# Emission order from a planned time of each operation instead of each stage, matmul kind changes in the planner's clock, and 17 + 23 work buffers instead of 15 + 24

## The chip, the cores and the metric

The kernel runs on one core of one Trainium2 chip. The metric is the device time of one execution in microseconds (us), as the median of several runs of the same program. The engines are named as in the profile: PE is the matrix engine, PEld its weight loads, DVE the vector engine, ACT the scalar engine, POOL the GpSimd engine, and SP the sync engine, which here does nothing but issue DMAs.

## The reference

One layer of a hybrid encoder over a sequence of 512 tokens with a model width of 1024, everything in float32. Cut to what is computed:

```python
h = rmsnorm(x, mix_norm)
p = h @ w_in                                   # 1024 -> 9248 columns
rx, ry, qkv, z, ba, gates = split(p)
y_rnn = rglru_branch(rx, ry, ...) @ w_rnn_proj # conv, two gated scans (forward, backward), gelu gate
y_dn  = deltanet_branch(qkv, z, ba, ...) @ w_dn_proj
g_rnn, g_dn = split(sigmoid(gates))
x = x + (g_rnn * y_rnn + g_dn * y_dn) @ w_out
h = rmsnorm(x, ffn_norm)
gt, up = split(h @ w_gate_up)                  # 1024 -> 2 * 2816
x = x + (silu(gt) * up) @ w_down
return rmsnorm(x, final_norm)
```

`deltanet_branch` is a chunked gated delta rule for 8 heads and two directions. Within a chunk it solves a triangular system (`lhs = A + eye`), and it carries a 128 x 128 state per head and direction from chunk to chunk.

## The kernel before, in words

**How it computes.** Each float32 operand of a large product is split into two parts, a rounded one (`hi`, type float32r) and the rest (`lo`), and a product is three matmuls: hi x hi, hi x lo and lo x hi. These "float32r" matmuls have 512 or 256 columns. ACT makes `hi` (a cast) and DVE makes `lo` (a subtraction) from a raw weight tile that SP has loaded. The two largest parts of the feed-forward block, `gate_up` and `down_first`/`down_second`, and `w_out`, are Strassen-like products with 7 instead of 8 block products, for which DVE also forms sums of blocks. The triangular inverse in `dn_inverse` (L924) is made of small float32 matmuls with `tile_position`, on 32 x 32 and then on 64 x 64 pieces of the array; the delta rule itself (`dn_mats`, L884, and `dn_state`, L1008) uses plain float32 matmuls of 128 or 256 columns; transposes are matmuls with the identity. So PE sees four kinds of work: float32r matmuls, transposes, full-size float32 matmuls, and small float32 matmuls on parts of the array.

**`dn_inverse`, which the prediction returns to.** It runs once for each of four groups `g` of two heads. Each run issues four sets of small matmuls: `pr` (32 of 32 x 32, L963 to L969), then `px` (32) and `pz` (16), both 32 x 32 and both fed by the same tile `R`, which ACT makes from `pr` (L972 to L980), then `pr2` (16 of 64 x 64, L992) and `px2` (16 of 64 x 64, L999). Between one set and the next lies an ACT operation that reads the PSUM of the first, except between `px` and `pz`. In the trace each float32 matmul has two rows, so a set of 32 shows as 64.

**How the order is made.** Nothing is issued while `trunk` (L390) runs through the code. Every operation goes through a recorder (`Rec`, L325), which gives it an engine, a cost in ns from a formula by operation and size, its dependences and the tiles it touches, and hands it to `Plan.add` (L123). At the end `Plan.order` (L150) plays the whole program against a clock of its own: each engine that is free picks, among its operations whose dependences are done, the one with the lowest number in `when` (`pick`, L225); it is busy for the operation's cost; a dependent operation becomes ready after a lag from the table `LAG`. The sequence in which operations were picked is the order of emission on each engine, and each engine of the chip then executes its list strictly in that order.

**Where `when` comes from.** `spend` (L444) cuts the program into 216 stages. The list `TIMES` (L35) holds one hand-over number for each stage, in units of 100 ns, between -163526 and 246650. They are priorities and not clock times. An operation's `when` is its stage's number plus an offset inside the stage (L154 to L161), so all operations of a stage, say all small matmuls of one `dn_inverse`, stand together.

**Tile promises.** Most tiles come from pools with a fixed number of buffers: `t2` (tag of `two`, 2 KB in each partition, `N2` buffers), `t4` (tag of `four`, 4 KB in each partition, `N4` buffers), `wraw` and `wx` (weights, 4 each), and three tags of PSUM banks, `mm` (3), `ax` (3) and `st` (2). An operation that needs a new tile can be picked only when `slots` (L192) allows it: a buffer must be free, and no more may be handed out than leaves room for the tiles with an earlier first use, as judged by `first` and `last` (L167 to L174), the lowest and highest `when` of the operations that touch a tile.

**The queues.** SP issues nearly all loads in the planned order and waits at each for the buffer it writes into. PE has no second queue: what stands in front of its list and is not ready holds everything behind it.

Of the kernel before, what the change touches and what calls it, by code (L numbers as in the profile page):

```python
# [14 lines left out]
P = 128  # L15
# [16 lines left out]
WARM = 3400  # L32
RELEASE = 200
LOOK = 40
TIMES = [  # L35
# [14 lines left out]
]  # L50
ENGINES = ("PE", "DVE", "ACT", "POOL", "SP")
N2, N4, NW = 15, 24, 4
# [7 lines left out]
class Plan:  # L60
# [9 lines left out]

    def __init__(self, nc):
        self.nc = nc
        self.ops = []
        self.where, self.bases = [], []
        self.t = self.base = 0.0
        self.stage = 0
        self.tags = {}
        self.tile_tag = {}
        self.hist = {}
        self.keep = set()  # L80
        self.extra = ()
        self.admit = ()
# [40 lines left out]
    def add(self, eng, fn, outs, ins, cost, tail=0.0, table=None):  # L123
# [23 lines left out]
        self.where.append((self.stage, round(1e3 * (self.t - self.base))))  # L147
        self.bases.append(round(1e3 * self.base))

    def order(self):  # L150
# [4 lines left out]
        when = []  # L155
        for (s, d), b in zip(self.where, self.bases):
            if s < len(TIMES):
                b, b0 = TIMES[s] * 100, b
            elif TIMES:
                b += max(TIMES) * 100 - b0  # L160
            when.append(b + d)  # L161
# [6 lines left out]
        for i, o in enumerate(ops):  # L168
            key = (when[i], i)
            for name in o[3]:  # L170
                if name in self.tile_tag:
                    uses[name] = uses.get(name, 0) + 1
                    first[name] = min(first.get(name, key), key)
                    last[name] = max(last.get(name, key), key)  # L174
# [14 lines left out]
        pe_end, cold = 0, WARM  # L189
# [53 lines left out]
        while True:  # L243
            for e in ENGINES:
# [17 lines left out]
                if e == "PE":  # L262
                    if now - pe_end > 3000:
                        cold = 0
# [60 lines left out]
class Rec:  # L325
# [5 lines left out]
    def __getattr__(self, op):  # L331
        real = getattr(self.real, op)

        def call(*a, **kw):
# [14 lines left out]
            elif e == "PE":  # L349
# [3 lines left out]
                cols = elems(a[1]) if op == "matmul" else P  # L353
                if op == "transpose":
# [1384 lines left out]
```

## Time and profile before

| | |
|---|---|
| median of 3 runs | 1052.06 us (1051.90 to 1052.31) |
| span of the profiled execution, first to last instruction | 1051.0 us |
| of the runs' time outside such a span (median less span) | 1.06 us |
| PE busy | 1037.1 us, 99% |
| PEld busy | 905.0 us, 86% |
| DVE busy | 869.5 us, 83% |
| ACT busy | 706.7 us, 67% |
| granted PE clock, mean | 0.999 |
| read from memory, written | 121.12 MB, 12.09 MB |

How to read the rows that follow: a row of the timeline has the start in us from the span's first instruction, the length, the engine, the line, the operation, what it writes and reads (`mm<-hh,wx`), for PE the piece of the array used (`128*128`, `32*32`), the output's shape, and the number of instructions merged into the row; in brackets, how long the engine sat idle before it and what ended that. All operations are issued from the recorder's one line, L384, so the line number tells nothing here and groups are told apart by tile names and shapes. Tiles are named by their tag: `t` stands for `t2` and `t4`, `ax`, `mm` and `st` for PSUM banks, `na` for the delta rule's matrices and later the residual. Matmuls overlap in the pipe, so a matmul's own length in the trace is longer than the time it takes from PE; that is read from the distance between starts.

### The profile page before, as it was taken

The page shows a single profiled execution, that of the slowest core. Times are in us where ns is not written, and L with a number is a line of the kernel's source. Part 1 is how long each engine was busy: PE and PEld are TensorE (multiplying, and loading weights), DVE is VectorE, ACT ScalarE, POOL GpSimd, SP SyncE. Part 2 cuts the span into 40 slices and gives each one's busy share as a digit, 9 for nine tenths or more (in the row PEclk, how much of TensorE's full clock was granted, in tenths as well). Part 3 has the DMA queues.
Part 4 walks back from the last instruction along what each step waited for, and adds up shares of the span by engine and source line. Part 5 has one row for each costly group of instructions (what it writes and reads, how often), then busy time and mean ns, then how long its engine had stood idle before and what let it go on. Part 6 is the DMA issues. An engine that isn't in the chain of part 4 may idle for free.

```text
span 1051.0 us, 17876 instructions
## 1 busy us (share of the span) xinstructions
PE 1037.1 (99%) x6707; PEld 905.0 (86%) x6707; DVE 869.5 (83%) x1626; ACT 706.7 (67%) x1287; POOL 75.7 (7%) x133
## 2 busy tenths in 40 slices
PE   8999999999999999999999999999999999999997
PEld 7888788888888987887888798889999999998886
DVE  7769989669794697489469657999999898989997
ACT  7799989787537877686875644668544454556574
POOL 2000000204100220211021000000000000000000
PEclk9999999999999999999999999999999999999999
DMA  9622222245233256559536564688453644336532
GB/s 278 196 79 81 61 75 75 71 112 148 81 100 91 73 144 150 158 133 218 122 76 145 169 172 140 197 256 292 129 171 102 200 139 130 109 110 207 197 123 80
DMA packets 180854, 146.95 MB, mean 140 GB/s; under 512 B 6784, under 2 KB 161552, under 8 KB 180768
## 3 DMA queue, kind: packets, MB, share of 16 engines
q1 hardware_dynamic: 175840, 129.95, 41.8%
q0 software_dynamic: 3744, 12.72, 6.5%
q10 hardware_dynamic: 1184, 3.15, 0.8%
q8 instruction: 52, 0.85, 0.3%
q14 instruction: 34, 0.28, 0.1%
HBM read 121.12 MB, written 12.09 MB: 127 GB/s over the span
## 4 chain that ended last, share of the span: by engine, by line
PE 86%; DVE 8%; ACT 2%; DMA 2%; issue 1%; SPq 1%; ACTq 0%; DVEq 0%
PE mm L384 49%; PE ax L384 23%; PE st L384 15%; DVE t L384 6%; ACT t L384 1%; DVE na L384 1%; DVE wx L384 1%; SPq L384 1%; DMA t<-in_w_down_dram 1%; DMA wraw<-in_w_in_dram 1%; DMA gain2r<-in_ffn_norm_dram 0%; ACT wx L384 0%; ACT ax L384 0%; ACTq L384 0%; ACT na L384 0%
## 5 line engine op out<-in xcount | busy, mean ns | idle before, releaser
L384 PE MATMUL mm<-hh,wx 128*128 128x512 f32 (+2 forms) x1280 | 368.8, 363 | 0.1
L384 DVE TENSOR_TENSOR t<-t,t 128x512 fp32r<-128x512 f32 (+25 forms) x501 | 249.3, 511 | 30.3 <-ACT t L384 20.7
L384 PEld LDWEIGHTS mm<-hh,wx 128*128 128x128 f32 (+1 forms) x1280 | 230.4, 188 | 35.4 <-ACT wx L384 0.7
L384 PE MATMUL mm<-hl,wx 128*128 128x512 f32 (+2 forms) x648 | 228.6, 362 | 0.0
L384 ACT CAST wx<-wraw 128x1024 fp32r<-128x1024 f32 (+3 forms) x139 | 129.9, 937 | 90.6 <-PE mm L384 32.9
L384 PE MATMUL ax<-t,t 128*128 128x512 f32 (+3 forms) x1134 | 156.9, 292 | 1.2 <-DVE t L384 1.2
L384 DVE TENSOR_TENSOR wx<-wraw,wx 128x1024 fp32r<-128x1024 f32 (+3 forms) x115 | 120.7, 1051 | 35.5 <-PE mm L384 16.8
L384 PEld LDWEIGHTS ax<-t,t 128*128 128x128 f32 (+1 forms) x1134 | 123.0, 161 | 21.6 <-issue 2.2
L384 PEld LDWEIGHTS mm<-hl,wx 128*128 128x128 f32 (+1 forms) x648 | 121.7, 188 | 16.8
L384 ACT CAST t<-t 128x512 fp32r<-128x512 f32 (+2 forms) x148 | 94.1, 653 | 44.5 <-DVE t L384 36.1
L384 PE MATMUL mm<-t,wx 128*128 128x512 f32 x480 | 116.6, 394 | 0.0
L384 PEld LDWEIGHTS mm<-t,wx 128*128 128x128 f32 x480 | 89.0, 188 | 18.4 <-issue 0.2
L384 DVE SCALAR_TENSOR_TENSOR t<-mm,par,t 128x511 f32<-128x511 f32 (+1 forms) x108 | 80.2, 744 | 20.9 <-ACT t L384 19.7
L384 ACT ACT_TABLE_LOAD x64 | 82.1, 1283 | 5.0 <-DVE t L384 2.3
L384 PE MATMUL mm<-t,t 128*128 128x256 f32 (+1 forms) x420 | 79.8, 330 | 0.1
L384 ACT ACTIVATE t<-t 128x128 f32<-128x128 f32 (+4 forms) x86 | 47.5, 559 | 41.0 <-DVE t L384 39.3
L384 PEld LDWEIGHTS mm<-t,t 128*128 128x128 f32 x420 | 63.8, 190 | 7.2 <-DVE t L384 0.5
L384 PE MATMUL st<-hh,wx 128*128 128x512 f32 (+1 forms) x224 | 67.7, 375 | 0.0
L384 ACT CAST t<-wraw 128x1024 fp32r<-128x1024 f32 (+1 forms) x55 | 49.2, 894 | 18.3 <-DMA wraw<-in_w_gate_up_dram 7.2
L384 DVE TENSOR_TENSOR t<-wraw,t 128x1024 fp32r<-128x1024 f32 (+1 forms) x55 | 56.3, 1023 | 5.3 <-ACT t L384 5.1
L384 PEld LDWEIGHTS st<-hh,wx 128*128 128x128 f32 x224 | 41.2, 188 | 7.6
L384 PE MATMUL st<-hl,wx 128*128 128x512 f32 (+1 forms) x112 | 41.5, 375 | 0.0
(195 smaller groups left out, 1519.1 us busy)
## 6 DMA issues: line engine op xcount, KB each, us to landing
wraw<-in_w_in_dram SPq DMA_DIRECT2D x72, 512.0 KB, 4.1
wraw<-in_w_gate_up_dram SPq DMA_DIRECT2D x44, 512.0 KB, 4.1
wx<-wraw POOLq DMA_DIRECT2D x24, 512.0 KB, 5.3
wraw<-in_w_out_dram SPq DMA_DIRECT2D x12, 512.0 KB, 4.5
wraw<-in_w_rnn_proj_dram SPq DMA_DIRECT2D x16, 384.0 KB, 3.5
t<-in_w_down_dram SPq DMA_DIRECT2D x11, 512.0 KB, 5.9
sums<-t SPq DMA_DIRECT2D x11, 512.0 KB, 5.0
wraw<-sums SPq DMA_DIRECT2D x11, 512.0 KB, 3.6
```

The costliest lines, as they stand in the source:

```text
L384: self.plan.add(e, lambda: real(*a, **kw), outs, ins, cost, tail, table)
```

## The change

The code that computes is untouched; the same 9123 operations are recorded in the same sequence. What differs is the planner.

- `TIMES`, with 216 numbers, gives way to `PLAN`, with 9123 numbers in units of 50 ns from 0 to 26830, one for each operation; `when` is that number. Stage and offset are no longer recorded.
- `first` and `last` of a tile are no longer the lowest and highest `when`. A pass through the dependences, in order of `when` among what is ready, gives each operation a rank, and a tile's first and last rank are used.
- Matmuls get a kind, kept where ACT's operations keep their table: 0 for float32r, 1 for a transpose, 2 for full-size float32, 3 for float32 on a part of the array. Where a matmul follows one of another kind, the planner's clock adds the entry of `TURN`, in ns: 95 from any other kind to kind 3, and from kind 3 back 215 to float32r, 100 to a transpose and 50 to full-size float32. `pick` itself does not look at kinds.
- Two cost formulas change: a small matmul of 64 columns costs 67 instead of 76 ns, and the slow DVE transpose is told by the number of dimensions of its operands instead of by its size.
- `N2` becomes 17 (from 15) and `N4` 23 (from 24). Together they keep 126 KB of each partition, as before.

```diff
-TIMES = [
-    -162283, -159297, -163526, -108037, -92752, -158970, -94346, -59098, 168648, -70151, -72611, -51972, -22916,
...
-]
+PLAN = """
+4054 7177 4989 4992 6589 4992 6593 2272 7050 2718 0 2823 4601 4293 4247 5798 5866 5860 5903 5818 5891 6158 6049 5989
...
+26810 26811 26825 26402 26821 26410 26830
+"""
 ENGINES = ("PE", "DVE", "ACT", "POOL", "SP")
-N2, N4, NW = 15, 24, 4
+N2, N4, NW = 17, 23, 4
...
+    TURN = ((0, 0, 0, 95), (0, 0, 0, 95), (5, 5, 0, 95), (215, 100, 50, 0))
...
-        when = []
-        for (s, d), b in zip(self.where, self.bases):
-            if s < len(TIMES):
-                b, b0 = TIMES[s] * 100, b
-            elif TIMES:
-                b += max(TIMES) * 100 - b0
-            when.append(b + d)
+        when = [50 * int(t) for t in PLAN.split()]
...
         uses, first, last = {}, {}, {}
-        for i, o in enumerate(ops):
-            key = (when[i], i)
-            for name in o[3]:
+        todo, heap = list(left), []
+        for i in range(n):
+            if not todo[i]:
+                heapq.heappush(heap, (when[i], i))
+        rank = 0
+        while heap:
+            i = heapq.heappop(heap)[1]
+            for name in ops[i][3]:
                 if name in self.tile_tag:
                     uses[name] = uses.get(name, 0) + 1
-                    first[name] = min(first.get(name, key), key)
-                    last[name] = max(last.get(name, key), key)
+                    first.setdefault(name, 2 * rank)
+                    last[name] = 2 * rank + 1
+            rank += 1
+            for u in users[i]:
+                todo[u] -= 1
+                if not todo[u]:
+                    heapq.heappush(heap, (when[u], u))
...
                 if e == "PE":
+                    c += self.TURN[mode][o[6]]
+                    mode = o[6]
                     if now - pe_end > 3000:
...
+                table = 1 if op == "transpose" else 0 if not four_ else 3 if elems(a[0]) <= 64 and a[0].shape[0] < P else 2
                 if op == "transpose":
                     cost = 110
                 elif four_:
-                    cost = 22 if cols == 32 else 76 if cols == 64 else n * 4 / 2.4 + 10
+                    cost = n * 4 / 2.4 + 10 if table == 2 else 22 if cols == 32 else 67
...
                 elif op == "transpose":
-                    cost = 68 + (2.0 if n > 512 else 1.1) * n
+                    cost = 68 + (2.05 if len(list(ins[0].ap)) > 3 or len(list(out.ap)) > 3 else 1.1) * n
```

More of the change, by code (lines that the diff above doesn't have):

```diff
@@ L73, in __init__ @@
         self.ops = []
-        self.where, self.bases = [], []
         self.t = self.base = 0.0
@@ L146, in add @@
         self.ops.append((eng, fn, deps, touched, round(cost), round(1.25 * tail), table, self.t))
-        self.where.append((self.stage, round(1e3 * (self.t - self.base))))
-        self.bases.append(round(1e3 * self.base))
     def order(self):
@@ L188, in order @@
         table = None
-        pe_end, cold = 0, WARM
+        pe_end, cold, mode = 0, WARM, 0
         result, start = [], {}
```

477 rows, old and new, of tables (PLAN, TIMES) are left out of this document.

## The prediction

> **What bounds the kernel now.** I read the page's head first, then the table of stretches, then PE's waits.
>
> ```profile
> span 1051.0 us, 17876 instructions
> PE 1037.1 (99%) x6707; PEld 905.0 (86%) x6707; DVE 869.5 (83%) x1626; ACT 706.7 (67%) x1287; POOL 75.7 (7%) x133
> ```
>
> PE is busy 1037.1 of 1051.0 us. An order can shorten only the 13.9 us in which PE is idle, and that part of its busy time which is not work but turning from one kind of matmul to another. So the question is where the 13.9 us lie. In the table of stretches each row has the stretch, its length, busy time (and instructions) of PE, PEld, DVE, ACT, POOL, then clock and DMA:
>
> ```profile
> 0.00:9.77 9.77, 6.40 (x33) 5.99 (x34) 4.90 (x16) 5.51 (x11) 7.04 (x21) 1.00 0.79 275
> 9.77:25.00 15.23, 13.62 (x100) 11.99 (x100) 13.29 (x31) 13.85 (x31) 0.00 (x0) 1.00 1.11 278
> 25.00:320.00 295.00, 294.99 (x1363) 244.40 (x1363) 247.51 (x360) 226.42 (x343) 21.55 (x30) 1.00 0.35 99
> 320.00:635.00 315.00, 313.93 (x2515) 266.55 (x2514) 214.28 (x568) 228.95 (x509) 46.23 (x81) 1.00 0.56 139
> 635.00:940.00 305.00, 303.75 (x2235) 289.69 (x2234) 284.57 (x484) 165.56 (x290) 0.87 (x1) 1.00 0.52 160
> 940.00:1044.00 104.00, 104.00 (x468) 86.26 (x467) 101.82 (x163) 64.55 (x103) 0.00 (x0) 1.00 0.49 159
> 1044.00:1051.10 7.10, 0.37 (x4) 0.17 (x2) 3.17 (x11) 1.85 (x5) 0.00 (x0) 0.85 0.53 192
> ```
>
> Idle of PE by stretch: 3.37 before the first product at 9.77; 1.61 up to 25; 0.01 in the next 295 us; 1.07 in the stretch of the four delta-rule groups (320 to 635); 1.25 in 635 to 940 (output projection, gate and up); nothing in 940 to 1044; 6.73 in the tail behind the last matmuls. The clock is 1.00 while PE works, so nothing is to be had there. The waits say who ended these idle times (total, times, longest):
>
> ```profile
> PE ax L384 <- DMA gain1r<-in_mix_norm_dram: 2.9, 1, 2.9
> PE ax L384 <- DVE t L384: 2.3, 3, 1.2
> PE mm L384 <- DVE hl L384: 1.3, 2, 0.8
> PE mm L384 <- ACT hh L384: 0.2, 1, 0.2
> PE ax L384 <- ACT ax L384: 0.2, 1, 0.2
> ```
>
> Of 6.9 us of waits the first 2.9 is the very first load, ahead of which there is no work. About 4 us remain. That the rest of the busy time is dense is seen in the chain, whose longest pieces are steady runs (start, us, what, matmuls):
>
> ```profile
> 277.53 45.33 PE mm L384 x200
> 812.36 4.32 PE ax L384 x36
> ```
>
> 45.33 / 200 is 0.227 us for a 512-column matmul, 4.32 / 36 is 0.120 for one of 256. A rule of the Trainium skill speaks against reading "99%" as the end: Perfetto Trace Analysis, section Identifying the Most-Contended Engine, calls matmul busy share a poor measure and has one look at the share of weight loads. By it there would be 14% of headroom (86% on the page); the two steady rates, which have no gap to close, say that an order finds none of it.
>
> **Terms of the change. First, the small matmuls.** PE's timeline shows visits to kind 3 between float32r runs (start, length, form, count):
>
> ```profile
> 322.89 0.75 PE L384 MATMUL ax<-t,na 32*32 32x32 f32 x64
> ...
> 324.70 0.75 PE L384 MATMUL ax<-t,t 32*32 32x32 f32 x64
> 325.38 2.56 PE L384 MATMUL mm<-t,wx 128*128 128x512 f32 x10
> 327.87 0.69 PE L384 MATMUL ax<-t,t 32*32 32x32 f32 x32
> 328.50 0.73 PE L384 MATMUL mm<-t,wx 128*128 128x512 f32 x2
> ...
> 419.95 0.75 PE L384 MATMUL ax<-t,t 32*32 32x32 f32 x64
> 422.90 0.69 PE L384 MATMUL ax<-t,t 32*32 32x32 f32 x32
> 500.56 1.02 PE L384 MATMUL ax<-t,t 32*32 32x32 f32 x96
> 501.51 0.50 PE L384 MATMUL mm<-hh,wx 128*128 128x512 f32 x1
> 503.01 1.52 PE L384 MATMUL mm<-hh,wx 128*128 128x512 f32 x6
> 504.46 1.15 PE L384 MATMUL ax<-t,na 64*64 64x64 f32 x32
> 505.54 0.97 PE L384 MATMUL mm<-hh,wx 128*128 128x512 f32 x3
> 506.34 0.39 PE L384 MATMUL mm<-hl,wx 128*128 128x512 f32 x1
> 591.54 1.02 PE L384 MATMUL ax<-t,t 32*32 32x32 f32 x96
> 598.09 1.15 PE L384 MATMUL ax<-na,t 64*64 64x64 f32 x32
> ```
>
> Around a visit: six matmuls from 503.01 should take 1.36 and the visit starts after 1.45, so 0.09 going in; three from 505.54 should take 0.68 and take 0.80, so 0.12 coming out. Inside there is a fixed part too: 64 rows take 0.68 (324.70 to 325.38), 32 take 0.63 (327.87 to 328.50), 96 together 0.95 (500.56 to 501.51). So `px` and `pz` as two visits cost 0.68 + 0.63 + 0.21 more of turning, 1.52, and as one 0.95: **a needless visit costs 0.57 us**. Groups 0 and 1 split the two sets (64 + 32), groups 2 and 3 don't (96). There are 18 visits from 322.89 to 598.09, 5 + 5 + 4 + 4. Four a group is the least, since ACT stands between the sets. In the diff the numbers (in us, 50 ns each) of the `pz` sets begin below those of `px` in three groups (the third has 798.95 us against 790.65), so `pz` no longer queues behind. I take both joins: 2 x 0.57 = **-1.1**, between -1.1 and a gain of nothing.
>
> All 18 visits have float32r on both sides. Coming out into a plain float32 matmul is planned as cheaper; no row shows it. Between 0 and 18 x 0.12 = -2.2 (the way out, gone altogether). I take 0, as `pick` doesn't look at kinds, and keep -1.9 for the 16 visits as an end.
>
> The Trainium skill, TensorEngine Tiling (Array Packing), section Key Properties, says that changing the tiling mode drains the engine. By that rule each visit pays twice, whatever its size, and the trace agrees with its 0.57. The diff's clock charges 0.31 (95 + 215 ns): it knows of the cost but prices it at little over half.
>
> **Second, the start.** SP now issues (start, length, tiles):
>
> ```profile
> 0.80 0.86 SPq L384 DMA_DIRECT2D t<-in_x_dram  x2
> 1.71 0.43 SPq L384 DMA_DIRECT2D wraw<-in_w_in_dram  x1
> 2.18 1.12 SPq L384 DMA_DIRECT2D t<-in_x_dram  x2
> 4.76 2.44 SPq L384 DMA_DIRECT2D wraw<-in_w_in_dram  x2
> ```
>
> `PLAN` puts the first three weight loads (306.20, 306.35, 307.55 us on its scale) ahead of the last two quarters of x (307.65, 307.75). All are ready at once, so the two x loads move behind one load of 128 KB and one of 512 KB. The DMA engines are full here (1.11, 278 GB/s), so x comes some 2.3 us later (640 KB / 278). PE needs these quarters last of all, and three weight tiles on the first half of the tokens are 3 x 24 matmuls of 0.120, 8.6 us of other work. I set the delay at 0 behind that cover; without it, it costs 2.3. In return PE starts with more weights to choose from while `hl` comes slowly (the 1.3 of waits above). Of 0.45 + 1.61 us idle I take **-0.6**, between -2.1 and +2.3.
>
> **Third, the waits in the middle.** 1.07 + 1.25 = 2.32 us. The longest one:
>
> ```profile
> 892.67 0.62 ACT L384 CAST t<-wraw 128x512 fp32r<-128x512 f32 x1 [3.63 <-DMA wraw<-in_w_gate_up_dram]
> 897.64 1.58 PE L384 MATMUL ax<-t,t 128*128 128x256 f32 x11 [1.18 <-DVE t L384]
> ```
>
> ACT sat 3.63 us for a weight load that SP issued late, and five us on PE paid 1.18 for it. A number for each operation can put such a load forward; one for a stage moves the whole stage. The two stretches with 0.01 and 0.00 idle show that a nearly waitless order exists for these costs. Between 0 and -2.3; I take **-1.5**, nearer to those rows. Late next is DVE: 101.82 of 104.00 after 940.
>
> **What I cost at nothing.** Turning between float32r, transposes and full-size float32 (planned at 0 to 5 ns). The tail of 6.73: `PLAN` keeps the sequence of the last eight DVE operations, with the last reciprocal behind the two scalings of another chunk. `marks` now also lists matmuls, as these have a kind; but each of them feeds a sigmoid that it listed already, so no wait is added. The two DVE and matmul formulas act only through the order. Two more `t2` and one fewer `t4`: no row shows a wait by pool, nearest is SP's wait for DVE to let go of a tile (total, times, longest):
>
> ```profile
> SPq L384 <- DVE t L384: 195.5, 72, 7.7
> ```
>
> I take 0, because PE idled 4 us while SP waited 195.5; the bad end is a rival below.
>
> **Sum.** -1.1 - 0.6 - 1.5 = -3.2 on the span of 1051.0, so 1047.8. The median of the runs, 1052.06, lies 1.06 above the span, which the order does not touch: 1047.8 + 1.06 = **1048.9 us**. Everything at its best is -1.1 - 1.9 - 2.1 - 2.3 = -7.4, or 1044.7.
>
> **Rivals.**
>
> *The gain is given back (0.17).* DVE becomes the wait: in 940 to 1044 it is busy 101.82 of 104.00 us, and PE has no slack there either. If the new order gains before 940 by pushing DVE's parts of later weights back, DVE enters this stretch with more to do and PE waits there. Against it: DVE has 20.4 us free in 635 to 940. It takes back from 2 to all of the 3.2: 1050.9 to 1052.1.
>
> *The small sets fall apart: slower (0.15).* With one number for a stage, a set of small matmuls stood together. With a number each, any float32r matmul that is ready and has a number between theirs goes between them. The diff's numbers do spread: the first group's `pr` set from 599.00 to 634.15 us, with 146 float32r matmuls numbered in between; the third group's `px` over 13 us with 60. The set holds together only where all its numbers lie before those of the float32r work then waiting, that is, where the chain comes late. Each split costs 0.57 on the chip and 0.31 in the plan, so the plan may accept some. It decides from 6 extra visits (3.4 us eat the gain); at 10, with the joins lost, it is -2.1 + 5.7 = +3.6, 1055.7. This is the case in which the drain rule above is the whole story.
>
> *One t4 buffer fewer: slower (0.10).* A raw tile is held longer, SP issues later, ACT and DVE get gate and up weights late. Each such event costs about the 1.18 seen once at 897.64, and there are 20 `gate_up` steps. Three more events undo the gain; five make it 1054.8.
>
> **Numbers.** The forecast has 0.58 with 1044.7 to 1050.4. From these: a measurement here can tell 0.2%, 2.1 us, from no change, so faster means below 1049.96 and slower above 1054.16. Of the 0.58, 0.54 is faster, 0.04 is same; of the giving back, 0.02 and 0.15; of the split sets 0.13 slower and 0.02 same; of the buffers 0.07 slower, 0.03 same. Sum: faster 0.56, same 0.24, slower 0.20. The range runs from the best of all terms, 1044.7, to the split sets at ten, 1055.7, beyond which and below which 2 in 10 are left.
>
> **What would show it.** Right: 16 visits to small forms, all `px` with `pz` as 96 rows; PE's waits after 25 us under 1 us in all; PE busy about 1 us less; the tail still 6.7. Wrong: more than 18 visits; a PE wait over 1 us for ACT or DVE; idle PE after 940; a first product later than 9.8, or PE waiting for `hh` around 20 us because x came late.

## The result, and the profile after

The changed kernel takes 1066.18 us (median of 4 runs, 1064.39 to 1068.55), the kernel before 1051.98 us beside it. The ratio is 1.0138, with a 95% interval of 1.0121 to 1.0154: 14.2 us slower, where 3.2 us less was forecast. The profiled execution of the changed kernel took 1067.54 us; its span, first to last instruction, is 1065.8. The head of its page:

```profile
span 1065.8 us, 17804 instructions
PE 1044.2 (98%) x6707; PEld 906.8 (85%) x6707; DVE 870.0 (82%) x1626; ACT 716.0 (67%) x1292; POOL 73.3 (7%) x133
```

PE does the same 6707 matmuls and is busy 7.1 us longer (1037.1 before), and idle 21.6 us instead of 13.9. The table of stretches (columns as in the prediction; the first edge is the first product, the last ones the end of the matmuls):

```profile
0.00:10.79 10.79, 6.40 (x33) 5.91 (x34) 5.21 (x16) 5.73 (x12) 7.14 (x21) 1.00 0.89 226
10.79:25.00 14.21, 12.37 (x97) 11.60 (x98) 11.44 (x28) 10.56 (x24) 0.00 (x0) 1.00 0.95 279
25.00:320.00 295.00, 292.66 (x1339) 240.18 (x1338) 246.00 (x355) 231.16 (x352) 17.89 (x32) 0.99 0.36 99
320.00:635.00 315.00, 309.43 (x2455) 260.74 (x2454) 207.41 (x539) 225.04 (x487) 47.35 (x79) 0.99 0.56 136
635.00:940.00 305.00, 303.92 (x2206) 287.99 (x2205) 280.62 (x494) 168.00 (x299) 0.87 (x1) 1.00 0.53 164
940.00:1059.00 119.00, 119.00 (x585) 100.15 (x584) 116.44 (x188) 73.33 (x116) 0.00 (x0) 1.00 0.43 142
1059.00:1066.00 7.00, 0.48 (x4) 0.27 (x3) 2.84 (x11) 2.14 (x5) 0.00 (x0) 0.74 0.62 222
```

Idle of PE is now 4.39 us before the first product (3.37 before), 1.84 to 25 us (1.61), 2.34 in 25 to 320 (0.01), 5.57 in 320 to 635 (1.07), 1.08 in 635 to 940 (1.25), none to the end of the matmuls, and 6.52 behind them (6.73). So the middle (25 to 940 us), where 1.5 us were to be gained, lost 6.7: 9.0 us of idle in place of 2.3. PE's waits (total, times, longest) name many causes with one wait each:

```profile
PE ax L842 <- issue: 3.7, 1, 3.7
PE ax L842 <- DMA gain1r<-in_mix_norm_dram: 3.0, 1, 3.0
PE mm L842 <- DVE hl L842: 1.8, 3, 1.1
PE st L842 <- DVE wx L842: 1.4, 1, 1.4
PE mm L842 <- ACT wx L842: 1.3, 2, 0.8
PE ax L842 <- DVE t L842: 1.3, 1, 1.3
PE mm L842 <- ACT t L842: 0.9, 1, 0.9
```

The longest, "issue", is one in which PE waited for no other engine. PE's timeline around it, in group 1:

```profile
429.40 0.75 PE L842 MATMUL ax<-t,na 32*32 32x32 f32 x64
...
431.44 1.19 PE L842 MATMUL ax<-t,t 32*32 32x32 f32 x88
436.37 0.33 PE L842 MATMUL ax<-t,t 32*32 32x32 f32 x8 [3.73 <-issue]
...
437.78 1.97 PE L842 MATMUL ax<-t,na 64*64 64x64 f32 x32
```

The joined `px` and `pz` set of 96 rows stops after 88, stands still for 3.73 us, and the 64-wide set behind it takes 1.97 instead of the 1.15 of the kernel before: half clock.

The second thing to see is on ACT, which PE's waits don't show. ACT's waits for transfers, the first rows, before:

```profile
ACT t L384 <- DMA wraw<-in_w_gate_up_dram: 7.2, 6, 3.6
ACT t L384 <- DMA wraw<-in_w_in_dram: 1.9, 2, 1.3
```

and after:

```profile
ACT t L842 <- DMA wraw<-in_w_gate_up_dram: 14.7, 13, 3.6
ACT wx L842 <- DMA wraw<-in_w_in_dram: 12.7, 9, 2.9
ACT wx L842 <- DMA wraw<-in_w_gate_up_dram: 11.6, 2, 7.5
```

Added up over all rows of that view, ACT waits for transfers 19.7 us in 18 waits before, and 57.3 us in 40 waits after. The planner's own clock says the same: of the 272 SP transfers whose first user is ACT or DVE, 41 land under 0.3 us ahead of that use in the order before, 69 in the changed one; the median lead falls from 5.8 to 3.1 us. In the changed order more weights are taken up as they land. One thing speaks against reading too much into this: 33.8 of ACT's 57.3 us (15.0 of the 19.7 before) lie in 635 to 940 us, where PE's idle did not rise.

A number used from here on: the time on the chip less the planner's own end (the instant at which its loop has done the last operation). It is 1051.98 - 1039.3 = 12.7 us for the kernel before and 1066.18 - 1042.7 = 23.5 us for the changed one. The planner itself gives the new order 3.4 us more, the chip another 10.8. The two distances are not quite alike: the planner of the kernel before does not price its turns between matmul kinds, that of the changed one does.

### The profile page after: what moved, and what is told of

Read it like the earlier page. It is cut to its first block, busy times and chain, and to the rows that moved or that the text cites. A ratio compares the mean times of both kernels' runs of the same rounds, so it can differ in the third digit from the quotient of the medians.

```text
span 1065.8 us, 17804 instructions
## 1 busy us (share of the span) xinstructions
PE 1044.2 (98%) x6707; PEld 906.8 (85%) x6707; DVE 870.0 (82%) x1626; ACT 716.0 (67%) x1292; POOL 73.3 (7%) x133
## 4 chain that ended last, share of the span: by engine, by line
PE 78%; ACT 7%; DVE 5%; DMA 4%; issue 2%; ACTq 0%; SPq 0%; DVEq 0%; POOLq 0%
PE mm L842 44%; PE ax L842 22%; PE st L842 13%; ACT t L842 4%; DVE t L842 3%; DVE wx L842 1%; DMA wraw<-in_w_in_dram 1%; ACT wx L842 1%; ACT L842 1%; DMA wraw<-osums 1%; DMA osums<-wraw 1%; DMA wx<-wraw 1%; ACT na L842 1%; DMA t<-osums 0%; DMA wraw<-in_w_dn_proj_dram 0%
## 5 line engine op out<-in xcount | busy, mean ns | idle before, releaser
L842 PE MATMUL mm<-hh,wx 128*128 128x512 f32 (+2 forms) x1280 | 379.4, 365 | 0.9 <-ACT wx L842 0.8
L842 DVE TENSOR_TENSOR t<-t,t 128x512 fp32r<-128x512 f32 (+17 forms) x501 | 251.0, 513 | 26.4 <-ACT t L842 16.4
L842 PEld LDWEIGHTS mm<-hh,wx 128*128 128x128 f32 (+1 forms) x1280 | 233.5, 190 | 37.0 <-ACT wx L842 1.6
L842 PE MATMUL ax<-t,t 128*128 128x512 f32 (+3 forms) x1134 | 172.6, 291 | 4.2 <-issue 3.7
L842 PEld LDWEIGHTS ax<-t,t 128*128 128x128 f32 (+1 forms) x1134 | 126.9, 161 | 24.2 <-issue 4.6
L842 PE MATMUL mm<-t,wx 128*128 128x512 f32 x480 | 123.4, 396 | 1.4 <-ACT t L842 0.9
L842 PE MATMUL mm<-t,t 128*128 128x256 f32 (+1 forms) x420 | 92.1, 329 | 0.0
L842 PEld LDWEIGHTS mm<-t,t 128*128 128x128 f32 x420 | 69.1, 190 | 7.1
L842 PE MATMUL st<-hh,wx 128*128 128x512 f32 (+1 forms) x224 | 70.2, 377 | 1.4 <-DVE wx L842 1.4
L842 POOL TENSOR_SCALAR_AFFINE_SELECT t<-t 128x512 f32<-128x512 f32 x32 | 24.7, 775 | 271.3 <-DMA t<-gcr 233.9
```

The costliest lines, as they stand in the source:

```text
L842: self.plan.add(e, lambda: real(*a, **kw), outs, ins, cost, tail, table)
```

## The experiments

Theories. *Late code*: the single stall of 3.73 us and the half clock behind it, some 6 to 7 us, are half of the loss (PE stands because its next instructions have not arrived). *No slack*: the table's order takes operands up as they are promised, so that any lateness reaches PE, and a wait that is taken away comes back elsewhere. Rivals of the prediction: one `t4` buffer fewer, and sets that fall apart. The second is out at once: there are 16 visits. The first stays untested: one more `t4` buffer (4 KB a partition) does not fit beside the 17 + 23, and with the old 15 + 24 the planner finds no order for this table.

The times of the changed order scatter by 4 us and more (1064.4 to 1068.6; the kernel before 1050.4 to 1053.3 in all its runs), so effects of 1 to 3 us are read from the traces, each of one execution. The runs are called e1 to e16 below.

**Code, by a shift of PE's stream (e1).**

```
+            if i == 2253:
+                for j in range(48):
+                    plan.again(2253 + j % 16)   # same matmul, one column
             plan.ops[i][1]()
```

> The changed kernel with its order untouched; ahead of the 64-wide set that began at 345.73 us, PE gets 48 extra matmuls of one column (into the set's own tile, overwritten by the set), 96 instructions more in PE's stream. Theory of the late code: PE's instructions arrive in blocks of 256, and the block that ends inside group 1's joined set (429.4 to 432.4 us) was used up in 2.8 us, before the next had been fetched. 96 instructions later in the stream that block holds matmuls of 0.227 us as well and lasts 6 to 8 us: the idle of 3.73 us at 436.37 goes, the half clock after it (437 to 441 us, some 3 us of PE time) too, the extra matmuls cost 0.6 to 1.0 us; 1066.2 - 3.7 - 3.0 + 0.8 = about 1060.3 us, unless the blocks at 514 and 602 us (5.6 and 3.2 us by my count after the shift) come late in their turn. Rival: the idle belongs to the place in the order (a transfer, a PSUM bank, a wait that the trace doesn't name): it stays at the same matmul of the set with 3 to 4 us, and the time is 1067 us.

Measured 1069.74 us. The set of 96 no longer stops; the stall has moved on by about the shift, into the next set, and a second one appears at 608 us (1.83 us):

```profile
431.79 1.25 PE L848 MATMUL ax<-t,t 32*32 32x32 f32 x96
...
433.64 0.91 PE L848 MATMUL ax<-t,na 64*64 64x64 f32 x22
437.50 0.56 PE L848 MATMUL ax<-t,na 64*64 64x64 f32 x10 [2.95 <-issue]
```

So it belongs to PE's stream of instructions and not to a place in the order; that the shift would clear it was wrong. Page part 3 has the queue that brings this code:

```profile
q8 instruction: 52, 0.85, 0.3%
```

52 packets of 16 KB for 13,414 matmuls and weight loads, 258 each. From 429.40 to the stop PE ran 64 + 5 + 88 matmuls with as many weight loads, 314 instructions in 3.2 us, more than a packet holds. The packet for which it waited began at 433.76 and took 1.00 us; PE went on 1.6 us after it had landed. In the seven such stalls of the changed kernel and the first five runs it went on 1.3 to 1.6 us after the landing. Counted from the start, PE had begun 4801 or 4802 matmuls and weight loads when it went on, in the changed kernel, in e2 to e5 and in the other plans e12, e14 and e15, and 5058 and 7618 in e1: each time 193 or 194 more than a multiple of 256. This ties the stall to the blocks of code, whatever the order. The Trainium skill (Runtime: NRT & Kernel Launch, section Instruction fetch mechanics) describes blocks of 256 instructions, read ahead by a queue of the engine's own; the trace agrees. It also says that the fetch is hidden by the pace of issue; here it isn't, 3.73 us of PE stand open.

**One wait, by one place in DVE's queue (e2).**

```
+        todo = move(todo, [1803], 2033)   # low half of wx443, ahead of two others
```

> The changed kernel; one DVE operation, the low half of a weight tile (wx443), is emitted ahead of the dn_mats and rg_rest operations that stood before it, so it can begin some 1.5 us earlier (248.9 instead of 250.45 us). Theory of the new wait: PE's wait of 1.44 us at 251.69 is this one queue position; it goes, and with it the eight matmuls at 0.427 instead of 0.227 us behind it (1.6 us): 1066.2 - 3.0 = 1063.2 us, and PE's slip against the planner's clock between 240 and 262 us grows by under 1 us instead of 3.7. Rival, no slack anywhere: the two operations that are now 1.2 us later are waited for in their turn within the next 20 us, and the time stays at 1065 to 1067 us.

Measured 1067.33 us. The wait at 251.69 is gone, and PE waits 1.02 us at 250.17 for the next `wx` of DVE. Matmul for matmul PE is 4.2 us ahead of the changed kernel's trace at 428 us, and 1.0 behind it at 705, after waits of 1.88 us at 617.7 and 1.85 at 700.5, which there are 0.69 and under 0.2. This is what the rival, no slack, said of the time, but the gain at 428 us is not this edit's. In e4 and e5 below, which leave this place as it was, the same wait is 0.28 and 0.32 us (1.50 in e1); they are 4.8 and 4.1 us ahead at 428 us and level with the changed kernel at 705. So the wait changes from execution to execution, and what these three had gained by 612 us they had given back by 705.

**The start (e3).**

```
+        todo = move(todo, [67, 68], 129)   # last quarters of x ahead of the 2nd weight
```

> The changed kernel; SyncE's first loads go back to the order of the kernel before: both last quarters of x ahead of the second weight load (they were issued at 6.58 and 8.40 us, they would be at about 2.2 and 2.8 us). Everything else in the changed order. Theory of the start: the second quarter of x no longer shares the transfer with two more weights (first transposes on it at 9.4, before 8.66 us), and DVE and ACT no longer wait for the late quarters (16.57 and 15.24 us): PE's slip at 60 us falls from 4.3 to about 2.3 us, 1066.2 - 2.0 = 1064.2 us. Rival: the casts of the two weights, now later in the transfer, stand ahead of the hh and hl writes on ACT (9.96 us) and wait instead: the start is the same or longer, 1066 to 1068 us.

Measured 1069.47 us. The rival's mechanism again, on ACT and then on PE:

```profile
11.77 0.41 ACT L842 CAST wx<-wraw 128x256 fp32r<-128x256 f32 x1 [2.62 <-DMA wraw<-in_w_in_dram]
```

```profile
12.61 0.49 PE L842 MATMUL mm<-hh,t 128*128 128x256 f32 x1 [2.60 <-ACT hh L842]
```

The load is late now, its cast stands ahead of the `hh` writes on ACT, and PE waits for these.

**The order inside the joined sets (e4).**

```
+        for a in (2174, 2948, 3756, 4598):
+            run = range(a, a + 48)
...
+            todo = done + [a + 1, a, *run[2:]] + [i for i in todo[k:] if i not in run]
```

> The changed kernel; within each of the four joined px and pz sets (96 rows of 32x32 matmuls) the matmuls stand in the order of the program, px and pz in alternation, instead of the 16 of pz first and then the 32 of px. Theory of the shuffled sets: each joined set falls from 1.4 to the 1.15 us that the joined set at 500.56 us took in the kernel before, so PE is about 0.3 us shorter per set, 1.2 us in all: 1065.0 us; since group 1's set then ends its block of code a little earlier, the idle at 436.37 us may grow by as much as it gains there (0.3 us). Rival: what a set costs is its number of rows and the two turns of kind, not its order: 1066.2 us, no difference that can be measured.

Measured 1069.78 us. The sets do get shorter; the changed kernel first, then this one:

```profile
339.70 1.26 PE L842 MATMUL ax<-t,t 32*32 32x32 f32 x96
340.89 0.73 PE L842 MATMUL mm<-t,wx 128*128 128x512 f32 x2
```

```profile
334.74 1.02 PE L842 MATMUL ax<-t,t 32*32 32x32 f32 x96
335.69 0.73 PE L842 MATMUL mm<-t,wx 128*128 128x512 f32 x2
```

From the start of the set to the next matmul 1.19 us became 0.95, for all four about 1 us. The time doesn't show it: the code stall is 4.30 us here, and idle of PE in all is 16.0 us (gaps between matmuls; 12.3 in the changed kernel).

**The transfers around the late code (e5).**

```
+        todo = move(todo, [3564], 3565)   # a write of 512 KB, one load later
```

> The changed kernel with one SyncE transfer moved: the 512 KB write of sums to DRAM that it issued at 427.99 us is issued one load later, after 431 us. What the four runs before showed: wherever the late block of code fell, PE went on 1.3 to 1.6 us after the block's packet had landed, and the packet itself began 3.6 to 4.7 us after PE had crossed into its last block there, against 0.5 to 0.7 us at the dense set near 339 us, where no transfer was under way. Theory of the queue for transfers: at 430 us a PoolE store, this write and a weight load (three times 512 KB) are in flight and the code's packet stands behind them; without the write it begins 1 to 2 us sooner, the idle in group 1's set falls from 3.7 (2.9 to 4.3) to between 1.5 and 2.5 us, and the time by as much: about 1064.5 us, within what these runs scatter. Rival: the delay of the packet is PE's own (its request goes out late, when the sequencer has run dry): idle and lateness stay at 3 to 4 us.

Measured 1068.16 us; the packet of code came 3.5 us late and PE idled 3.11 us. The transfers behind the write moved up: when PE crossed into its last block, a store by POOL and a weight load were in flight, and the code was as late. That clears this write, and tells nothing of transfers at large: inconclusive.

**One part alone: the joins, in the kernel before (e6).**

```
+        for a, b in ((2174, 2222), (2948, 2996)):
+            k = todo.index(a)
+            todo = [i for i in todo[:k] if not a <= i < b] + list(range(a, b)) \
+                 + [i for i in todo[k:] if not a <= i < b]
```

> The kernel before, with one part of the change alone: in groups 0 and 1 the 16 matmuls of pz are put beside the 32 of px (one set of 96 rows in the order of the program), so two visits fewer, 16 instead of 18; everything else as before. Theory of my first term: two visits at 0.57 us go, 1051.9 - 1.1 = 1050.8 us. Rival of the late code: the denser set uses up its block sooner and an idle of 1 to 4 us opens in it, as in the changed kernel: 1052 to 1056 us.

Measured 1050.77 us against 1052.04 us, ratio 0.9987 (0.9978 to 0.9997): 1.27 us less, where 1.1 was worked out. Groups 0 and 1:

```profile
324.12 1.02 PE L384 MATMUL ax<-t,t 32*32 32x32 f32 x96
325.07 3.03 PE L384 MATMUL mm<-t,wx 128*128 128x512 f32 x12
...
418.84 1.02 PE L384 MATMUL ax<-t,t 32*32 32x32 f32 x96
419.79 1.19 PE L384 MATMUL mm<-hh,wx 128*128 128x512 f32 x4
```

0.95 us a set and no stall. This agrees with the first term, count and price, though the interval allows a gain of 0.3 to 2.3 us; it is faster than both kernels. By the drain rule of the Trainium skill (TensorEngine Tiling (Array Packing), Key Properties) a visit costs whatever its size; two visits fewer and 1.27 us less agree with that.

**Lateness of every weight.** Two burdens, each on both kernels (e7 and e8, e10 and e11).

```
+                to, src = a[0][0:16], a[1][0:16]
+                self.plan.add(e, lambda: (real(to, src), real(*a, **kw)), outs, ins, cost, tail, table)
```

> The changed kernel, each of its 231 weight loads preceded on SyncE's queue by a second load of its first 16 partitions (64 KB, overwritten by the load itself), so every weight lands roughly 0.5 us later; order untouched. Theory of no slack: the changed order takes weights up as they land (the planner's own clock has 69 of 272 loads land under 0.3 us ahead of their first use, 41 before; ACT waits for transfers 57.3 us in 40 waits, 19.7 us in 18 before), so lateness goes straight through ACT's queue to PE: at least 8 us slower than itself, 1074 us or more, and at least one and a half times what the same burden costs the kernel before. Rival: its losses are the late code and half clock alone; it loses what the kernel before loses, within 2 us.

> The kernel before with the same burden on each weight load (64 KB more ahead of it, each weight some 0.5 us later). Theory of no slack in the changed order: this one has more, so it loses 2 to 6 us: 1054 to 1058 us. Rival: both lose the same, whatever that is.

Measured 1322.55 us, and 1249.15 us for the kernel before. The burden was eight times what I meant: the second transfer to the same place waited for the first to land, some 4 us per weight. The sizes were missed, and so was the ratio: the changed kernel lost 256 us, the kernel before 197, 1.30 where at least 1.5 was expected. So, without a byte to spare for waiting:

```
+                parts = [(a[0][p:q], a[1][p:q]) for p, q in ((0, 16), (16, P))]
+                self.plan.add(e, lambda: [real(*x, **kw) for x in parts], outs, ins, cost, tail, table)
```

> The changed kernel, each of its 231 weight loads issued as two transfers, 16 partitions and then the other 112: no byte more, but one more issue on SyncE (some 0.45 us) ahead of most of the load, so the weights land roughly 0.5 us later. (The burden tried before was 4 us per load, since the second transfer to the same place waited for the first; it cost the kernel before 197 us and the changed one 256 us.) Theory of no slack: the changed order passes lateness on more than the one before, in the ratio 1.3 or above: 4 us or more beyond what the kernel before loses under the same burden. Rival: both lose the same within 2 us.

> The kernel before with the same split of its weight loads, 0.5 us later each. Theory of no slack in the changed order: it loses 2 to 10 us, at least 4 us less than the changed kernel loses. Rival: the same loss within 2 us.

Measured 1087.34 and 1066.28 us: the changed kernel loses 21.2 us, the kernel before 14.4 (more than the 10 that I allowed it). The difference, 6.8 us, and the ratio, 1.47, are those that no slack expected; as the runs scatter by 8 and 4 us, the difference is known to some 4 us only. The burden is not quite the same either: the main part of a `w_in` load took 4.8 us to land where the whole took 3.9 (median) in the changed kernel, 4.6 for 4.1 in the kernel before.

Where the time goes is read by setting each profiled execution, matmul for matmul, against that of the same kernel unburdened. The changed kernel is 1.4 us later at 25 us, 2.4 at 635 and 15.7 at the end; the kernel before 2.0, 4.6 and 11.1. So the changed order is the more sensitive one behind 635 us, where the change itself lost nothing. Between 25 and 635 us, where it lost most, the burden cost it 1.0 us, and the kernel before 2.6. The pair shows an order with less slack; it does not show that late weights made the 14.2 us.

**Without the crowd in group 1 (e9).**

```
+            if 2948 <= i < 2996 or 3010 <= i < 3026:
+                if i in (2948, 2949, 3010):
...
+                    nc.tensor.matmul(plan.sets[1][k][:, 0:n], sl[0:1, :], f(hh[0:1, 0, 0:n]), start=True, stop=True)
+                continue
             plan.ops[i][1]()
```

> The changed kernel without the crowd in which code came late: of group 1, the joined px and pz set (96 rows) and the 64-wide set after it are left out, each of their three tiles is filled with zeros by one matmul instead (so that group's inverse is not computed; ACT's copies and everything after them run as before), and PE's stream is 244 instructions shorter, about one block, so later sets lie in their blocks as before. Own work: 96 rows at 1.4 us and the 64-wide set at 1.3 us go, three fp32 matmuls of 256, 256 and 512 columns come (0.43 + 0.43 + 0.85 us): 1.0 us less. Theory of the late code: with it go the idle of 2.9 to 4.3 us and some 3 us at half clock: 1066.2 - 1.0 - 3.7 - 3.0 = about 1058.5 us. Theory of no slack: PE comes to 445 us that much sooner, and waits for ACT's weights and transfers instead, between 560 and 710 us above all (0.7 to 2.2 us each, as in the runs where it came there 4 us sooner): 1062 to 1066 us, with 3 us or more of new waits of over 0.6 us behind 445 us.

Measured 1063.45 us, 2.7 less than the changed kernel. Little of it is work left out: the matmuls that fill the tiles took 1.05 and 1.05 us (1.7 in all were expected), the two sets take 1.19 and 1.08 where nothing stops them. No stall for code is left. In its place, PE's longest waits:

```profile
PE st L843 <- ACT t L843: 4.1, 3, 1.8
PE ax L843 <- DMA gain1r<-in_mix_norm_dram: 3.0, 1, 3.0
PE ax L843 <- DVE t L843: 1.7, 3, 1.1
```

Where the 4.1 us come from is seen on ACT, which stands at the same transfers in both; the changed kernel, then this one:

```profile
618.60 0.62 ACT L842 CAST t<-t 128x512 fp32r<-128x512 f32 x1 [1.59 <-DMA t<-osums]
620.36 1.05 ACT L842 CAST wx<-wraw 128x1024 fp32r<-128x1024 f32 x1 [0.53 <-DMA wraw<-in_w_in_dram]
```

```profile
611.54 0.62 ACT L843 CAST t<-t 128x512 fp32r<-128x512 f32 x1 [2.94 <-DMA t<-osums]
615.16 1.04 ACT L843 CAST wx<-wraw 128x1024 fp32r<-128x1024 f32 x1 [2.40 <-DMA wraw<-in_w_in_dram]
```

ACT came here 5 to 7 us sooner, and waits 1.4 and 1.9 us longer for the same two. Matmul for matmul PE is 8.2 us ahead of the changed kernel at 618 us (4.0 of them from before the sets), 4.9 at 705 and 3.5 at 1000.

The half clock was taken out only in part, since PE ran at half clock here too, without any stall (0.50, the third number from the end):

```profile
431.02:434.44 3.42, 3.42 (x11) 2.35 (x9) 0.75 (x1) 3.36 (x6) 0.00 (x0) 0.50 0.82 269
```

With 3.73 us of stall and 0.7 of the 2.4 us of half clock gone, some 4.4 us were taken out, and about 2.5 stay gained, within a scatter of 4 us. Late code is a real part of the loss, but short of half of it.

**Which part of the change (e12 to e15).** Four more plans, by the planner itself, each with one thing changed:

```
+                    c += self.TURN[mode][o[6]]     # e13: kernel before + turns and cost formulas
-                    c += self.TURN[mode][o[6]]     # e14: changed kernel without them
-                    done = bus + 908
+                    done = bus + 1400              # e12; 1900 in e15
```

> The changed kernel, planned again with one number of the planner's clock changed: each transfer counts as landed 0.49 us later (1400 for 908 ns), so whatever uses a weight is put that much behind its landing. The planner's own end becomes 1050.7 us, from 1042.7. Theory of no slack: the chip ran the changed order 23.9 us behind the planner's clock because so much was put right at the landing; with half a microsecond in hand it falls behind by 18 us at most: 1068.5 us or less. Rival: it falls behind for other reasons, as much as before: 1050.7 + 23.9 = 1074.6 us.

> The kernel before with one part of the change alone: the turns between matmul kinds and the changed cost formulas are in the planner's clock, orders and promises still from the table of stage times, 15 + 24 buffers. The planner's own end is 1064.0 us then (17 visits), 24.7 us later than without the prices. Time on the chip over the planner's end was 12.7 us for the kernel before, of which about 10 are the turns it did not price. Theory: pricing is honest, so the chip comes 2 to 6 us behind the planner's end: 1066 to 1070 us; the loss is the plan's, and stays without the new table. Rival: pricing does not make the clock truer, 1064.0 + 12.7 = 1076.7 us.

> The changed kernel with the other part alone: the planned time of each operation, promises and 17 + 23 buffers as changed, but no turns and the old cost formulas in the planner's clock. Its own end is 1044.7 us (24 visits of the small matmuls). Theory: the table's order has no slack, and the turns come on top unpriced: 1044.7 + 12 to 23.5 (what the changed kernel ran behind) + 24 visits at 0.57 us = 1070 to 1082 us. Rival: it is the pricing that costs, and the table alone runs 12.7 us behind like the kernel before: 1057.4 us.

> The changed kernel planned with landings 0.99 us later than its own clock had them (1900 for 908 ns; 1400 gave a planner's end of 1050.7 us and 1065.95 us on the chip, 15.3 behind, against 23.5 behind for the change itself). The planner's end is 1057.6 us. Theory of no slack: the more is held in hand, the less the chip falls behind, 8 to 11 us here, so the same 1066 to 1069 us for the third time: what the planner promised with a landing of 908 ns was never there to be had. Rival: past 1400 the chip gains no more, 1057.6 + 15.3 = 1072.9 us.

| kernel | planner's end | chip | behind | visits | ACT waits for transfers, us (times) |
|---|---|---|---|---|---|
| before | 1039.3 | 1051.98 | 12.7 | 18 | 19.7 (18) |
| e13, pricing alone | 1064.0 | 1076.66 | 12.7 | 17 | 18.8 (18) |
| e14, table alone | 1044.7 | 1070.07 | 25.4 | 24 | 58.6 (36) |
| changed: both | 1042.7 | 1066.18 | 23.5 | 16 | 57.3 (40) |
| e12, both, landing + 0.49 us | 1050.7 | 1065.95 | 15.3 | 20 | 47.7 (32) |
| e15, both, landing + 0.99 us | 1057.6 | 1070.29 | 12.7 | 20 | 28.7 (23) |

Three things follow. The loss and the late weights come with the table (or with the 17 + 23 buffers, which go with it in all these runs): e14 has both; the late weights are not in e13, whose loss is of another kind. Pricing was needed by the table (eight visits fewer, 3.9 us less from e14 to the changed kernel, at 0.57 us each 4.6), but alone it upsets the old order: ACT waits for transfers no longer in e13 than before, and PE waits 22.8 us in all, 13.2 of them for weights that ACT casts. Its expected 2 to 6 us behind were wrong, the rival's 1076.7 right. And the planner can be given 0.49 us more for each landing, which costs 8.0 us by its clock, at no cost on the chip, with four visits more: by this measure those 8 us were promised and never there. At 0.99 us the chip does pay (1070.29, between theory and rival).

**A mended kernel before (e16).** The joins, and two places in DVE's queue.

```
+        todo = move(todo, [285], 58)      # low half of the first weight behind five hl
+        todo = move(todo, [8276], 8094)   # a gate_up sum ahead of a low half
```

> The kernel before with both joins of group 0 and 1 (1050.8 us when run alone), and two DVE operations moved: the low half of the first weight tile goes behind five hl operations at the start (PE waited 0.85 us for the first of them at 10.9 us), and in gate_up the sum that PE waited for at 895 us (0.7 to 1.2 us) goes ahead of the low half before it, 0.6 us sooner. Theory: there is slack around these places, 0.7 and 0.5 us are kept: 1049.6 us. Rival: what is moved back is waited for in its turn, 1050.8 us.

Measured 1050.87 us, ratio 0.9990 (0.9981 to 0.9999); the joins alone gave 1050.77. The wait at the start moved from 10.9 to 13.53 us and grew to 1.02, the one at 895 us is 0.68 us (0.71 in the run with the joins alone). What was moved back was waited for in its turn: these two moves found no free time in the kernel before either. The joins are the whole gain that these runs found.

## Why the prediction was wrong

**First term, the small matmuls: the count held, the price agrees.** 16 visits, all four joins, and 1.27 us (0.3 to 2.3) for two where 1.1 was put. Two things were not in it. The table also shuffles the matmuls inside a set (1.19 for 0.95 us), about 1 us for the four. And joining them makes the crowd that outran its code; in the kernel before the same joins do not.

**Second, the start: the cover was the wrong thing, the sign stays open.** First product 10.79 instead of 9.77 us. "PE needs these quarters last of all", with 8.6 us of matmuls to cover them, holds for PE and not for DVE's queue:

```profile
13.93 1.21 DVE L842 TENSOR_TENSOR t<-wraw,t 128x1024 fp32r<-128x1024 f32 x1
16.57 0.69 DVE L842 SCALAR_TENSOR_TENSOR t<-t 128x512 f32<-128x512 f32 x1 [1.43 <-DMA t<-in_x_dram]
...
17.18 0.48 DVE L842 SCALAR_TENSOR_TENSOR hl<-ax,gain,hh 128x256 fp32r<-128x256 f32 x1
```

DVE stands at the late quarter, and behind it in its queue are `hl` operations of the first half, for which PE waits 1.08 us. In this execution idle up to 25 us rose by 1.25 us, to 6.24; the end that I kept, +2.3, was of the right kind. But the wait of 1.08 us is not in every execution: e1, e2, e4, e5 and e9 have the same start and idle 3.4 to 4.9 us up to 25 us, against 4.97 in the kernel before (4.45 in e6), with the first product at 9.9 to 10.4 us. The start is no sure part of the 14.2 us.

**Third, the waits in the middle: this step failed.** I took -1.5 us; PE's idle from 25 to 940 us rose by 6.7 instead, from 2.3 to 9.0, and to 10.5 to 13.1 in e1, e2, e4 and e5, which share the order but for the one edit. "A number for each operation can put such a load forward", I wrote. The one wait named, 1.18 us, is indeed gone. But the table's numbers do not put loads forward as such: they follow, some 300 us higher, the times at which the planner starts the operations (three quarters of them to within 3 us), so that more loads come where they land just in time by its clock. What opened in place of the wait: 3.73 us for code in the joined set of group 1, 1.44 us for a weight's low half late in DVE's queue, and waits for ACT of under 1 us.

How far late weights are behind this is in part argued. For it speak the distance to the planner's clock, 23.5 us, that shrinks to 15.3 and 12.7 as landings are priced later, and the 21.2 us for a burden that costs the kernel before 14.4; against it, that this burden and most of ACT's waits for transfers fall behind 635 us, where the change lost nothing. My reason, that nearly waitless stretches exist for these costs, took the planner's costs for the chip's.

**What I cost at nothing.** The tail held (6.5 us). PE's busy time was to fall by 1 us and rose by 7.1: about 4 us are half clock (below), 1 us the shuffled sets; the other 2 I have not pinned down, float32r matmuls now alternate with transposes 49 times instead of 35.

**The rivals.** The sets did not fall apart. Giving back was the right mechanism in the wrong place: not DVE after 940 us, where PE has no idle at all, but before it, between 612 and 705 us above all. "One `t4` buffer fewer" named late weights as the way to lose. The row that the prediction gave for it has grown, from 195.5 us in 72 waits:

```profile
SPq L842 <- DVE t L842: 327.1, 96, 19.4
```

It is 209.5 us in e13, with the old buffers and stage times, and 331.5, 294.8 and 284.3 in e14, e12 and e15, with the new ones. Buffers and table are not separated by these runs, so this rival stands; that e15, with the same 17 + 23, has half of ACT's waits for transfers says only that the buffers alone do not set them.

What stays open: how the 14.2 us divide between late weights, code and half clock, since what was taken out singly came back in whole or in part; and the share of the 17 + 23 buffers. ACT also loads its function tables 69 times instead of 64, at 1.28 us each; no run took that apart.

## What to carry to other kernels

A plan that puts every operand at its promised landing is only as good as the promise: count how many operands have less slack than the landings scatter, and compare it with the order that is to be replaced, before believing the planner's end. Before a wait is mended, see whether another execution of the same order has it at all. When waits are taken out one by one and the time stays, look at the slack, and at the stage in which it is missing: a burden that hurts in another stage than the change did proves little. A small, certain part of a large change (here two joins) is worth running alone on the old order.

## What the runs showed of the hardware

Code can come late: see above, 3.73 us when 314 instructions run in 3.2 us. Near 339.70 a set as dense did not stall; one weight load was in flight there (not none, as an expectation above has it), and the packet began about 0.6 us after PE had crossed into its last block, against about 4.1 us near 430, with three transfers in flight. That the transfers delay it was argued, and the run made to test it did not tell.

Behind two of PE's waits the clock fell for several microseconds. The granted clock is the third number from the end:

```profile
251.69:257.00 5.31, 5.15 (x14) 3.79 (x15) 5.31 (x10) 1.07 (x2) 0.44 (x1) 0.68 0.73 195
436.30:441.00 4.70, 4.63 (x45) 3.61 (x45) 0.00 (x0) 4.16 (x8) 0.00 (x0) 0.50 0.44 141
```

0.50 over 4.70 us behind the idle of 3.73, and 0.68 over 5.31 us behind one of only 1.44: 2.4 and 1.7 us of work lost, more than the second wait itself. The Trainium skill (TensorE: Matmul & The Clock Gate, Part 1) lets the clock fall after an idle window of about 3.4 us; 1.44 us sufficed here. But the wait alone does not decide it: the clock stayed at 1.00 behind 1.50 us at the same place in e1, behind 1.85 us at 700.5 in e2 and behind 2.09 us at 621.5 in e5, and it was 0.50 over the 3.41 us from 346.61 in e1, behind the 48 one-column matmuls and no such wait.

DVE was slower here while POOL worked: 1.11 us for a 512-column operation whose like took 0.68 at 239.39 us, before POOL began at 240.29. No run separates the two; beside it POOL was busy:

```profile
244.17 1.11 DVE L842 TENSOR_TENSOR t<-t 128x512 f32<-128x512 f32 x1
245.20 1.67 DVE L842 TENSOR_TENSOR t<-t,t 128x1024 f32<-128x1024 f32 x1
```

```profile
243.50 1.24 POOL L842 TENSOR_SCALAR_AFFINE_SELECT t<-t 128x512 f32<-128x512 f32 x1 [1.86 <-DMA t<-gcr]
```
